# Token-major b, k and v of an RWKV-7 mixer by 32x32 blocks on VectorE, with a different spacing of steps

## The chip, the core and the metric

The kernel runs on one core of a Trainium2 chip. TensorE (PE) multiplies, VectorE (DVE), ScalarE (ACT) and GpSimd (POOL) work on tiles in SBUF, SyncE (SP) issues loads. The metric is device microseconds of one execution, the median over the runs; lower is better.

## The reference

One layer of a decoder: an input projection feeds two mixers that run side by side, a sliding-window attention and an RWKV-7 time mixing; both are projected, gated and merged, and a SwiGLU feed-forward follows. All is float32, with 2048 tokens and 16 meta tokens, width 1024.

```python
u = rms_norm(h, norm_mix_g); proj = u @ w_in + b_in
y_attn = sliding_window_sink_attention(partial_rope(q), partial_rope(k), v, sinks)
y_rwkv = rwkv7_time_mix(p_rwkv, ...)
merged = gates[..., :D] * (y_attn @ w_br_attn) + gates[..., D:] * (y_rwkv @ w_br_rwkv)
h = h + merged @ w_o
f = rms_norm(h, norm_ffn_g)
h = h + (silu(f @ w_gate) * (f @ w_up)) @ w_down
# inside rwkv7_time_mix, for each token and head, with state S (64x64):
sa = S a_t
S = S * w_t + sa b_t + v_t k_t ;  y = S r_t
```

## The kernel before

**The dense work.** The 2048 tokens go in four blocks of 512. `phase_a(b)` makes the input projection, `phase_c(b)` the branch projections (`pb`), the output projection (`ph_o`), the feed-forward (`pg`, `pu`) and its return (`ph_d`). Each float32 product is made of three matmuls of 128x512. TensorE executes its instructions in the order in which the program issues them (`InOrder`); the other engines' queues are ordered by a scheduler when the program is built.

**The mixers** are Python generators that `tick()` moves on by one step (one `yield`) after every few dense matmuls. One step of one unit stands for about 18 dense matmuls on TensorE's queue. An RWKV unit `rwkv(i, j)` treats 256 tokens (four chunks of 64) of two heads; there are 32, and one for the meta tokens. A unit starts `LAG` = 14 steps after the one before it. Attention units `attn(ti)` treat 128 tokens of all heads and run one after another.

**What an RWKV unit does**, in the order of its steps: loads and shifts `rkv`; makes decays (`pc`, `pe`, `pi`) and the block-diagonal operand `bkd` (b and k, feature-major, written by VectorE at L730 and L731); makes the chunk matrices `pg` on TensorE; sends one of them through DRAM (`lt_d`, `lt`) to GpSimd, which inverts it in 62 operations (L772, L774, the tiles `pr` and `xv`). Then it turns `bkd` and v token-major: 8 transposes on TensorE into `pb`, which ScalarE copies to `bt`, and 2 into `pvv`, which VectorE and ScalarE copy to the block-diagonal `vd`. After `WAIT_INV` steps the inverses return through DRAM (`xt_d`, then `td`), VectorE turns two blocks of them (`tq`, L808), and TensorE completes them (`pq`, `pq2`) and runs the recurrence over the four chunks (`ch`, with `ud` and `sd` on VectorE, `rd` and `yt` on ScalarE). At the end `yt` is normalised, turned (`pyt`) and stored to `y_d`.

**What an attention unit does**: loads q, k, v and the rotated copies `qr`, `kr` by SP; one step later GpSimd rotates them (L945 to L947, and `roped`), `set_keys` splits the keys into `kw`, and `parts(0)` splits q into `qs` on ScalarE and VectorE (L955, L956); two steps later TensorE turns v (`pv`) and makes the scores (`psS`).

Of the kernel before, what the change touches and what calls it, by code (L numbers as in the profile page):

```python
# [19 lines left out]
F32 = mybir.dt.float32  # L20
F32R = mybir.dt.float32r
AF = mybir.ActivationFunctionType
# [5 lines left out]
P = 128  # L28
# [19 lines left out]
WAIT_INV = 9  # L48
# [30 lines left out]
def layer(ctx, tc, x, meta, w_in, w_br, w_o, w_gate, w_up, w_down, w2a, a2, g2, vecs, sinks, gfin,  # L79
          consts, rope, out):  # L80
    nc = tc.nc
    V, A, G, S = nc.vector, nc.scalar, nc.gpsimd, nc.sync
# [18 lines left out]
    T = InOrder()  # L101
# [8 lines left out]
    cp = pool("const")  # L110
    dp = pool("dram", space=DRAM)
    dn = pool("dense")
    mx = pool("mixer")
    psd = pool("psd", bufs=3, space=PSUM)
    psg = pool("psg", bufs=4, space=PSUM)
    psc = pool("psc", bufs=1, space=PSUM)

    def f32(ap):
        return ap.bitcast(F32)
# [22 lines left out]
    ident = cc("ident")  # L142
# [407 lines left out]
    bkd = cp.tile([P, 2, 4, P], F32, name="bkd")  # L550
    vds = [cp.tile([P, 4, P], F32, name=f"vd{q}") for q in range(2)]
    td = cp.tile([P, 4, P], F32, name="td")
    rd = cp.tile([P, P], F32, name="rd")
    ud = cp.tile([P, P], F32, name="ud")
    for t in (bkd, *vds, td, rd):
        G.memset(t, 0.0)
    gmask = cst[:, _CC["gstrict"][0]:_CC["gincl"][1]]

# [56 lines left out]
    n = TU // CH  # L615

    def rwkv(i, j):
# [3 lines left out]
        m = i is None  # L621
        uid = 4 * NU if m else 4 * i + j
        nm = f"{i}_{j}"
        t1 = lambda s, b=1: mx.tile([P, TU], F32, tag=s, bufs=b, name=f"{s}_{nm}")
        cv = lambda ap: ap.rearrange("p (c t) -> p c t", t=CH)
# [17 lines left out]
        rm, km, vm = (rkv[:, q] for q in range(3))  # L643
# [84 lines left out]
        for h in range(2):  # L728
            hb = slice(64 * h, 64 * h + 64)
# [13 lines left out]
        for x in range(2):  # L743
            pg = psg.tile([P, 512], F32, tag="pg", name=f"pg_{nm}_{x}")
# [29 lines left out]
            G.tensor_add(xv[:, :, r + 1:], xv[:, :, r + 1:], pr[:, :, :n_])  # L774
        yield

        bt = mx.tile([P, 2, n, P], F32, tag="bt", bufs=2, name=f"bt_{nm}")
        vd = vds[(uid + m) % 2]
        for x in range(2):
            pb = psg.tile([P, 512], F32, tag="pg", name=f"pb_{nm}_{x}")  # L780
            for c in range(n):
                T.transpose(pb[:, c * P:(c + 1) * P], bkd[:, x, c], ident)
            A.activation(bt[:, x], pb.rearrange("p (c f) -> p c f", f=P), AF.Copy)
            if x == 0:
                yield
        pvv = psg.tile([P, 512], F32, tag="pg", name=f"pvv_{nm}")
        for t in range(2):
            T.transpose(pvv[:, t * P:(t + 1) * P], vm[:, t * P:(t + 1) * P], ident)
        pvt = pvv[:, :2 * P].rearrange("p (t f) -> p t f", f=P)
        for q in range(2):  # L790
            for h in range(2):
                hb, qb = slice(64 * h, 64 * h + 64), slice(64 * q, 64 * q + 64)
                if q == h:
                    V.tensor_copy(vd[hb, q::2, hb], pvt[qb, :, hb])
                else:
                    A.activation(vd[hb, q::2, hb], pvt[qb, :, hb], AF.Copy)
        for _ in range(WAIT_INV):
            yield
        G.dma_start(xt_d[uid].rearrange("m (b c) i -> b m (c i)", c=4), xv.rearrange("p c i -> p (c i)"))
        lo, hi = [slice(64 * h, 64 * h + 32) for h in range(2)], [slice(64 * h + 32, 64 * h + 64) for h in range(2)]  # L800
        for h in range(2):
            for q, r32 in ((0, lo[h]), (1, hi[h])):
# [21 lines left out]
        for c in range(n):  # L824
# [8 lines left out]
            for h in range(2):  # L833
                hb = slice(64 * h, 64 * h + 64)
# [45 lines left out]
    def set_keys(k, cols):  # L880
        for g in range(2):
            gb = slice(64 * g, 64 * g + 64)
            for d in (gb, slice(64 - 64 * g, 128 - 64 * g)):
                A.activation(kw[d, g, 0, cols], k[gb], AF.Copy)
                V.tensor_sub(kw[d, g, 1, cols], k[gb], f32(kw[gb, g, 0, cols]))
# [6 lines left out]
    def roped(o, src, rot, cs, w, name):  # L892

        G.tensor_mul(src, src, cs[:, 0])
        G.tensor_mul(rot, rot, cs[:, 1])
        G.tensor_add(o, src, rot)
# [28 lines left out]
    def attn(ti):  # L925
# [7 lines left out]
        q = mx.tile([P, 4, P], F32, tag="q", bufs=1, name=f"q_{ti}")  # L933
# [6 lines left out]
        load_rot(kr, 4, 1, c0, P)  # L940
        vt = mx.tile([P, P], F32, tag="vl", bufs=1, name=f"vl_{ti}")
        S.dma_start(vt, proj_d[5][:, c0:c0 + P])
        yield
        b4 = lambda k: cs[:, k].unsqueeze(1).to_broadcast([P, 4, P])
        G.tensor_mul(q, q, b4(0))  # L945
        G.tensor_mul(qr, qr, b4(1))
        G.tensor_add(q, q, qr)  # L947
        roped(kl[:, 0], kl[:, 0], kr[:, 0], cs, P, ti)
        set_keys(kl[:, 0], own)

        def parts(g):
# [14 lines left out]
        for g in range(2):  # L966
            gb = slice(64 * g, 64 * g + 64)
            nm = f"{ti}_{g}"
# [58 lines left out]
    def tick():  # L1027

        turn[0] = (turn[0] + 1) % TURNS
        rs = [u for u in units if u[2] == "r"]  # L1030
        for u in list(units):
            if turn[0] != (0 if u[2] == "a" else 1 if len(rs) > 1 and u is rs[0] else 2):
                continue
            u[1] += 1
            if next(u[0], 0) == 0:
                units.remove(u)
        if todo_r and turn[0] == 2:
            i, j = todo_r[0]
            b = (i or 0) // 2
            young = min((u[1] for u in units if u[2] == "r"), default=LAG)  # L1040
            if young >= LAG - 3 and i not in asked and set(range(6, 9)) <= emitted[b]:
                asked.add(i)
                start("l", lora(i), b)
            if young >= LAG and i in loras and set(
                    range(9, 21) if i is None else range(PAIR0 + 3 * j, PAIR0 + 3 * j + 3)) <= emitted[b]:
                todo_r.pop(0)
                start("r", rwkv(i, j), b)
        if todo_a and turn[0] == 0 and not any(u[2] == "a" for u in units):
            ti = todo_a[0]
            b = (ti or 0) // 4  # L1050
            if set(range(6)) <= emitted[b]:
                todo_a.pop(0)
                start("a", attn_meta() if ti is None else attn(ti), b)
# [135 lines left out]
```

## Time and profile before

| | us |
|---|---|
| median of 3 runs (3372.03 to 3376.8) | 3375.84 |
| the profiled execution, its own time | 3377.94 |
| its span | 3376.0 |
| PE busy | 3256.3 (96%) |
| DVE busy | 1542.1 (46%) |
| ACT busy | 1163.2 (34%) |
| POOL busy | 1156.1 (34%) |

TensorE is busy in nearly the whole span; its idle time lies in waits that the trace names, and after a longer wait its granted clock is halved for a few microseconds.

### The profile page before, as it was taken

Reading aid. Unit: us, or ns where it says so; the run is one execution under the profiler, and the core shown is the slowest. Engines: PE = TensorE matmul, PEld = TensorE weight load, DVE = VectorE, ACT = ScalarE, POOL = GpSimd, SP = SyncE. Lnnn points to the kernel's source line nnn. Section 1 sums busy time; section 2 is a strip of 40 time slices with the busy share of each in tenths; the row PEclk is TensorE's granted clock in tenths of the full one; section 3 lists DMA queues with packets and bytes.
Section 4 is the critical chain, followed back from the end, with each engine's and each line's share of the span. In section 5 each row is a group of like instructions: output and inputs, shape, how many; then the busy total and the mean of one; then the engine's idle time right before and its main releaser. Section 6 shows DMA issues by size and latency. Waiting matters only on the chain.

```text
span 3376.0 us, 47237 instructions
## 1 busy us (share of the span) xinstructions
PE 3256.3 (96%) x16909; PEld 2681.2 (79%) x16909; DVE 1542.1 (46%) x3622; ACT 1163.2 (34%) x2863; POOL 1156.1 (34%) x2771
## 2 busy tenths in 40 slices
PE   7899999999999998999999999999999999999998
PEld 6777887787888777887787788887888888778887
DVE  3343233232332585666666644445654443542233
ACT  4354344443443455445443422233242221220001
POOL 1124434334344454554453433444333341000000
PEclk9999999999999999999999999999999999999999
DMA  7777666676666776666668555556755555855555
GB/s 262 273 261 241 209 226 211 190 227 197 223 210 215 242 260 206 234 235 234 231 237 280 176 170 174 179 181 201 263 171 177 171 177 176 288 179 191 196 191 181
DMA packets 229448, 721.46 MB, mean 214 GB/s; under 512 B 36333, under 2 KB 90989, under 8 KB 168286
## 3 DMA queue, kind: packets, MB, share of 16 engines
q1 hardware_dynamic: 158126, 516.15, 47.1%
q0 software_dynamic: 38736, 154.99, 12.9%
q10 hardware_dynamic: 32352, 47.31, 3.8%
q8 instruction: 133, 2.18, 0.3%
q14 instruction: 101, 0.83, 0.1%
HBM read 533.46 MB, written 184.82 MB: 213 GB/s over the span
## 4 chain that ended last, share of the span: by engine, by line
PE 60%; DMA 6%; DVE 3%; POOL 3%; ACT 2%; issue 2%; SPq 0%; POOLq 0%; DVEq 0%; ACTq 0%
PE pg L93 14%; PE pu L93 12%; PE ph_d L93 11%; PE pi L93 6%; PE pb L93 4%; PE ch L93 4%; PE ph_o L93 3%; DMA yl<-y_d 1%; PE ph_o_l L93 1%; POOL pr L772 1%; POOL xv L774 1%; DMA lt<-lt_d 1%; PE py L93 1%; PE pq L93 1%; DVE h L202 1%
## 5 line engine op out<-in xcount | busy, mean ns | idle before, releaser
L93 PE MATMUL pi<-act_u,w_in 128*128 128x512 f32 x3552 | 902.5, 402 | 10.5 <-DVE m L202 6.1
L93 PEld LDWEIGHTS pi<-act_u,w_in 128*128 128x128 f32 x3552 | 652.9, 191 | 144.0 <-issue 5.5
L93 PE MATMUL pg<-act_f,w_g 128*128 128x512 f32 x2112 | 533.7, 399 | 6.8 <-DVE act_f L202 6.8
L93 PE MATMUL pu<-act_f,w_u 128*128 128x512 f32 x2112 | 522.9, 395 | 0.0
L93 PE MATMUL ph_d<-w_d,mg_g 128*128 128x512 f32 x1920 | 472.5, 397 | 10.4 <-DVE h L202 10.0
L93 PEld LDWEIGHTS pg<-act_f,w_g 128*128 128x128 f32 x2112 | 388.4, 189 | 85.3 <-DVE act_f L202 9.0
L93 PEld LDWEIGHTS pu<-act_f,w_u 128*128 128x128 f32 x2112 | 388.9, 188 | 78.8 <-issue 1.0
L93 PEld LDWEIGHTS ph_d<-w_d,mg_g 128*128 128x128 f32 x1920 | 355.5, 189 | 85.9 <-DVE h L202 14.5
L772 POOL TENSOR_TENSOR pr<-xv,lt 128x124 f32<-128x124 f32 (+30 forms) x992 | 330.5, 333 | 248.9 <-DMA lt<-lt_d 176.8
L774 POOL TENSOR_TENSOR xv<-xv,pr 128x124 f32<-128x124 f32 (+30 forms) x992 | 341.1, 344 | 74.5
L202 DVE SCALAR_TENSOR_TENSOR h<-ph_d,h 128x512 f32<-128x512 f32 x320 | 218.9, 689 | 130.0 <-PE ph_d L93 128.3
L93 PE MATMUL pb<-ya,w_br 128*128 128x512 f32 x768 | 191.0, 400 | 1.0 <-DMA w_br<-wd_br 0.6
L93 PEld LDWEIGHTS pb<-ya,w_br 128*128 128x128 f32 x768 | 143.1, 191 | 30.9 <-DVE mg_m L202 1.0
L202 DVE SCALAR_TENSOR_TENSOR th<-th,pg 128x512 f32<-128x512 f32 x88 | 60.4, 687 | 214.6 <-ACT th L202 214.5
L93 PE MATMUL ph_o<-w_o,mg_m 128*128 128x512 f32 x576 | 144.2, 400 | 6.8 <-DVE h L202 3.8
L804 POOL DMA_DIRECT2D td<-xt_d x132 | 72.6, 557 | 225.4 <-PE ch L93 197.3
L202 ACT ACTIVATE th<-pg 128x512 f32<-128x512 f32 x88 | 52.6, 598 | 281.4 <-PE pg L93 281.0
L202 DVE TENSOR_TENSOR th<-th,pu 128x512 f32<-128x512 f32 x88 | 60.5, 687 | 183.8 <-PE pu L93 183.3
L243 POOL TENSOR_TENSOR ss_o<-ss_o,mhalf 128x1 f32<-128x1 f32 x16 | 9.4, 590 | 372.5 <-DVE ss_o L202 372.3
L755 POOL DMA_DIRECT2D lt_d<-g x128 | 71.2, 561 | 184.0 <-DVE g L750 182.0
L202 ACT ACTIVATE mg_g<-th 128x512 fp32r<-128x512 f32 x88 | 55.3, 628 | 222.6 <-DVE th L202 222.5
L93 PEld LDWEIGHTS ph_o<-w_o,mg_m 128*128 128x128 f32 x576 | 106.5, 190 | 31.3 <-DVE h L202 5.2
(356 smaller groups left out, 4512.1 us busy)
## 6 DMA issues: line engine op xcount, KB each, us to landing
w_in<-wd_in SPq DMA_DIRECT2D x111, 1024.0 KB, 5.5
w_g<-wd_g SPq DMA_DIRECT2D x66, 1024.0 KB, 5.0
w_u<-wd_u SPq DMA_DIRECT2D x66, 1024.0 KB, 5.0
w_d<-wd_d SPq DMA_DIRECT2D x60, 1024.0 KB, 5.0
wd_in<-w_in POOLq DMA_DIRECT2D x37, 1024.0 KB, 5.8
w_br<-wd_br SPq DMA_DIRECT2D x24, 1024.0 KB, 7.0
wd_g<-w_g POOLq DMA_DIRECT2D x22, 1024.0 KB, 5.2
wd_u<-w_u POOLq DMA_DIRECT2D x22, 1024.0 KB, 5.3
```

Of the source, the lines that this page charges most:

```text
L93: r = f(*p, **k)
L202: return f(*p, **k)
L243: G.tensor_tensor(ss[:rows, 3:4], ss[:rows, 2:3], mhalf[:rows, 0:1], op=ALU.pow)
L755: G.dma_start(lt_d[uid, m0:m0 + n].rearrange("c j i -> j c i"), g[r32, :, 0, o])
L772: G.tensor_mul(pr[:, :, :n_], xv[:, :, r:r + 1].to_broadcast([P, 4, n_]), lt[:, r, r + 1:].unsqueeze(1).to_broadcast([P, 4, n_]))
L774: G.tensor_add(xv[:, :, r + 1:], xv[:, :, r + 1:], pr[:, :, :n_])
L804: G.dma_start(td[r32, :, r32], xt_d[uid, m0:m0 + 4].rearrange("m j i -> j m i"))
```

## The change

The ten TensorE transposes of a unit and the copies out of PSUM are replaced by `V.transpose` of 32x32 blocks from SBUF to SBUF: 8 instructions for v and 16 for b and k, each over four chunks (32 partitions, 4x32 elements). `bt` becomes two fixed, zeroed tiles `bts`, used in turn. The step ahead of each half of `bt` stays within the unit's count up to the store of the inverses, and one step is added between that store and the loads of `td`. In the attention one step is added between the loads and the rotation, and two between the rotation and `set_keys` with `parts(0)`.

```diff
-    for t in (bkd, *vds, td, rd):
+    bts = [cp.tile([P, 2, 4, P], F32, name=f"bt{q}") for q in range(2)]
+    for t in (bkd, *vds, td, rd, *bts):
         G.memset(t, 0.0)
...
-        bt = mx.tile([P, 2, n, P], F32, tag="bt", bufs=2, name=f"bt_{nm}")
-        vd = vds[(uid + m) % 2]
+        bt, vd = bts[(uid + m) % 2], vds[(uid + m) % 2]
+        vc4 = cv(vm)
+        for h in range(2):
+            for r in range(2):
+                for q in range(2):
+                    rb, qb = (slice(64 * h + 32 * z, 64 * h + 32 * z + 32) for z in (r, q))
+                    V.transpose(vd[qb, :, rb], vc4[rb, :, 32 * q:32 * q + 32])
         for x in range(2):
-            pb = psg.tile([P, 512], F32, tag="pg", name=f"pb_{nm}_{x}")
-            for c in range(n):
-                T.transpose(pb[:, c * P:(c + 1) * P], bkd[:, x, c], ident)
-            A.activation(bt[:, x], pb.rearrange("p (c f) -> p c f", f=P), AF.Copy)
-            if x == 0:
-                yield
-        pvv = psg.tile([P, 512], F32, tag="pg", name=f"pvv_{nm}")
-        for t in range(2):
-            T.transpose(pvv[:, t * P:(t + 1) * P], vm[:, t * P:(t + 1) * P], ident)
-        pvt = pvv[:, :2 * P].rearrange("p (t f) -> p t f", f=P)
-        for q in range(2):
+            yield
             for h in range(2):
-                hb, qb = slice(64 * h, 64 * h + 64), slice(64 * q, 64 * q + 64)
-                if q == h:
-                    V.tensor_copy(vd[hb, q::2, hb], pvt[qb, :, hb])
-                else:
-                    A.activation(vd[hb, q::2, hb], pvt[qb, :, hb], AF.Copy)
-        for _ in range(WAIT_INV):
+                for r in range(2):
+                    for q in range(2):
+                        rb, qb = (slice(64 * h + 32 * z, 64 * h + 32 * z + 32) for z in (r, q))
+                        V.transpose(bt[qb, x, :, rb], bkd[rb, x, :, qb])
+        for _ in range(WAIT_INV - 1):
             yield
         G.dma_start(xt_d[uid].rearrange("m (b c) i -> b m (c i)", c=4), xv.rearrange("p c i -> p (c i)"))
+        yield
...
         S.dma_start(vt, proj_d[5][:, c0:c0 + P])
-        yield
+        for _ in range(2):
+            yield
...
         roped(kl[:, 0], kl[:, 0], kr[:, 0], cs, P, ti)
+        for _ in range(2):
+            yield
         set_keys(kl[:, 0], own)
```

**Place 1, TensorE's queue where unit (4, 3) makes its chunk matrices `pg`.** Unit (4, 2) is the one before it; `ph_o1` is dense work of block 1. Before:

```order
L93 MATMUL pb_1_7_1_18743<-ya_1_7_17969,w_br_1_7_18704 128x512 x3
L93 MATMUL ph_o1_7_0_0_18764<-w_o1_7_0_18762,mg_m1_4_18450 128x512 x3
L93 MATMUL pq2_4_2_0_18768<-td_118,tq_4_2_18656 32x32 x4
L93 MATMUL pq2_4_2_1_18769<-td_118,tq_4_2_18656 32x32 x4
L93 MATMUL ch_4_2_0_18782<-vd0_116,g_4_2_1_18083 128x128
L93 MATMUL ch_4_2_0_18782<-sd2_109,ar_4_2_17891 128x128
L93 MATMUL ch_4_2_0_18782<-vd0_116,bt_4_2_18218 128x128
L93 MATMUL pg_4_3_0_18790<-ar_4_3_18673,bkd_115 128x128 x4
L93 MATMUL pg_4_3_1_18802<-ar_4_3_18673,bkd_115 128x128 x4
```

Now:

```order
L93 MATMUL pb_1_7_1_18647<-ya_1_7_17785,w_br_1_7_18623 128x512 x3
L93 MATMUL ph_o1_7_0_0_18686<-w_o1_7_0_18684,mg_m1_4_18335 128x512 x3
L93 MATMUL pq_4_2_0_18690<-tq_4_2_18639,g_4_2_0_17872 32x32 x4
L93 MATMUL pq_4_2_1_18691<-tq_4_2_18639,g_4_2_0_17872 32x32 x4
L93 MATMUL pg_4_3_0_18702<-ar_4_3_18581,bkd_115 128x128 x4
L93 MATMUL pg_4_3_1_18714<-ar_4_3_18581,bkd_115 128x128 x4
```

From `pq` on, a unit stands one step later against the unit behind it: `pq` of (4, 2) now stands where its `pq2` stood, 36 dense matmuls behind `pc` of (4, 3) and no longer 18.

**Place 2, VectorE's queue where unit (4, 3) writes `bkd`.** `tq_4_2` are the two blocks of the unit before, for which `pq` of place 1 waits; `gst` and `yt` belong to unit (4, 1), `ptm` to the attention, `mt` to the dense work. Before:

```order
L808 STREAM_TRANSPOSE tq_4_2_18656<-td_118 32x128
L855 TENSOR_SCALAR gst_4_1_18710<-gst_4_1_18710 128x4
L723 TENSOR_TENSOR bv_4_3_18669<-rkv_4_3_18438,pbo_4_3_18666 128x256
L727 TENSOR_TENSOR ar_4_3_18673<-kn_4_3_18480,pe_4_3_18662 128x4x64
L732 TENSOR_TENSOR ar_4_3_18673<-rkv_4_3_18438,pe_4_3_18662 128x4x64
L734 COPY fc_4_3_18680<-pe_4_3_18662 128x4
L738 COPY pe0_4_3_18683<-pe_4_3_18662 128x1
L730 TENSOR_TENSOR bkd_115<-tw_4_3_18671,pi_4_3_18664 64x4x64
L731 TENSOR_TENSOR bkd_115<-kp_4_3_18552,pi_4_3_18664 64x4x64
L730 TENSOR_TENSOR bkd_115<-tw_4_3_18671,pi_4_3_18664 64x4x64
L731 TENSOR_TENSOR bkd_115<-kp_4_3_18552,pi_4_3_18664 64x4x64
```

Now:

```order
L732 TENSOR_TENSOR bkd_115<-kp_4_3_18459,pi_4_3_18572 64x4x64
L737 TENSOR_TENSOR fc_4_3_18588<-pe_4_3_18570 128x3
L819 TENSOR_SCALAR sd3_110<-sd3_110,pe0_4_3_18591 128x128
L1007 TENSOR_TENSOR ptm_14_1_18608<-ppm_14_1_18606,cst_80 128x512
L792 STREAM_TRANSPOSE bt1_122<-bkd_115 32x4x32 x4
L202 SCALAR_TENSOR_TENSOR mt_1_6_1_18613<-tg_1_6_1_18538,pb_1_6_1_18559 128x512
L792 STREAM_TRANSPOSE bt1_122<-bkd_115 32x4x32 x8
L842 SCALAR_TENSOR_TENSOR sd1_108<-ch_4_1_3_18510,fc_4_1_16794,sf_4_1_3_18516 128x128
L805 STREAM_TRANSPOSE tq_4_2_18639<-td_118 32x128 x2
L792 STREAM_TRANSPOSE bt1_122<-bkd_115 32x4x32 x2
L202 TENSOR_TENSOR mt_1_6_0_18557<-mt_1_6_0_18557,mt_1_6_1_18613 128x512
L792 STREAM_TRANSPOSE bt1_122<-bkd_115 32x4x32 x2
```

The scheduler puts most of the 16 transposes of `bkd` right behind its last write, and the older unit's `tq` behind 12 of them; before, `tq` stood ahead of `bkd`.

**Place 3, GpSimd's queue where attention unit 7 rotates q.** `pr` and `xv` are the inversion of an RWKV unit, with the operation's number behind the unit's. Before:

```order
L774 TENSOR_TENSOR xv_1_2_7705<-xv_1_2_7705,pr_1_2_4_7719 128x4x27
L772 TENSOR_TENSOR pr_1_2_5_7722<-xv_1_2_7705,lt_1_2_7703 128x4x26
L774 TENSOR_TENSOR xv_1_2_7705<-xv_1_2_7705,pr_1_2_5_7722 128x4x26
L772 TENSOR_TENSOR pr_1_2_6_7725<-xv_1_2_7705,lt_1_2_7703 128x4x25
L945 TENSOR_TENSOR q_7_7853<-q_7_7853,cs_7_7851 128x512
L774 TENSOR_TENSOR xv_1_2_7705<-xv_1_2_7705,pr_1_2_6_7725 128x4x25
L947 TENSOR_TENSOR q_7_7853<-q_7_7853,qr_7_7854 128x512
L772 TENSOR_TENSOR pr_1_2_7_7728<-xv_1_2_7705,lt_1_2_7703 128x4x24
```

Now:

```order
L773 TENSOR_TENSOR pr_1_3_30_8464<-xv_1_3_8372,lt_1_3_8370 128x4
L892 TENSOR_TENSOR kr_7_8861<-kr_7_8861,cs_7_8851 128x128
L775 TENSOR_TENSOR xv_1_3_8372<-xv_1_3_8372,pr_1_3_30_8464 128x4
L893 TENSOR_TENSOR kl_7_8860<-kl_7_8860,kr_7_8861 128x128
L795 DMA xt_d_79<-xv_1_3_8372 8x16x128
L769 DMA xv_2_0_9153<-in_consts 128x128
L943 TENSOR_TENSOR q_7_8853<-q_7_8853,cs_7_8851 128x512
L945 TENSOR_TENSOR q_7_8853<-q_7_8853,qr_7_8854 128x512
```

The rotation stood after the seventh of 31 rounds of the inversion of unit (1, 2), with `psS` of this attention unit 81 dense matmuls behind `pg` of (1, 2) on TensorE's queue; now it stands behind the whole inversion of (1, 3), and `psS` 264 dense matmuls behind that unit's `pg`.

## Rows read from the trace of the kernel before

**Rows 1.** The page, busy time of each engine, its share of the span, instructions

```profile
PE 3256.3 (96%) x16909; PEld 2681.2 (79%) x16909; DVE 1542.1 (46%) x3622; ACT 1163.2 (34%) x2863; POOL 1156.1 (34%) x2771
```

**Rows 2.** Waits of PE: what it waited for, us in total, times, longest

```profile
PE psS L93 <- DVE qs L956: 27.3, 9, 5.8
...
PE ph_d L93 <- DVE h L202: 10.0, 7, 4.5
PE psS L93 <- ACT kw L884: 7.1, 1, 7.1
PE pq L93 <- DVE tq L808: 6.9, 2, 5.2
...
PE ph_o L93 <- DVE h L202: 3.8, 2, 3.3
```

**Rows 3.** Groups by line and form on PE: busy, mean ns; the unit's transposes

```profile
L93 PE MATMUL pb<-cst,bkd 128*128 128x128 f32 x256 | 38.8, 275 | 0.0
...
L93 PE MATMUL pvv<-cst,rkv 128*128 128x128 f32 x64 | 12.2, 273 | 0.0
```

**Rows 4.** Timeline of PE, one burst of four transposes: start, length, instructions

```profile
2549.71 0.60 PE L93 MATMUL pb<-cst,bkd 128*128 128x128 f32 x4
```

**Rows 5.** Groups on ACT and DVE: the copies that empty those PSUM tiles

```profile
L783 ACT ACTIVATE bt<-pb 128x512 f32<-128x512 f32 x64 | 38.2, 596 | 120.9 <-PE pb L93 120.9
...
L796 ACT ACTIVATE vd<-pvv 64x128 f32<-64x128 f32 x64 | 17.4, 272 | 2.4 <-DVE vd L794 1.6
...
L794 DVE COPY vd<-pvv 64x128 f32<-64x128 f32 x64 | 18.4, 288 | 26.8 <-ACT vd L796 15.1 <-PE pvv L93 10.8
```

**Rows 6.** DVE, the only 32x32 transposes of before: their group, and one pair in the timeline

```profile
L808 DVE STREAM_TRANSPOSE tq<-td 32x128 f32<-32x128 f32 x64 | 19.0, 297 | 20.3 <-DMA td<-xt_d 19.2
...
2019.15 0.62 DVE L808 STREAM_TRANSPOSE tq<-td 32x128 f32<-32x128 f32 x2
```

**Rows 7.** Timeline of DVE and PE about one write of `bkd`

```profile
2535.07 0.41 DVE L730 TENSOR_TENSOR bkd<-tw,pi 64x256 f32<-64x256 f32 x1
2535.41 0.41 DVE L731 TENSOR_TENSOR bkd<-kp,pi 64x256 f32<-64x256 f32 x1
2535.83 0.42 DVE L730 TENSOR_TENSOR bkd<-tw,pi 64x256 f32<-64x256 f32 x1
2536.17 0.42 DVE L731 TENSOR_TENSOR bkd<-kp,pi 64x256 f32<-64x256 f32 x1
...
2532.47 0.61 PE L93 MATMUL pc<-cst,sig 128*128 128x130 f32 x4
...
2533.15 4.24 PE L93 MATMUL ph_d<-w_d,mg_g 128*128 128x512 f32 x18
...
2542.28 0.59 PE L93 MATMUL pq<-td,tq 32*32 32x32 f32 x16
```

**Rows 8.** Windows: length, then busy (instructions) of PE, PEld, DVE, ACT, POOL, clock, DMA

```profile
1097.20:1860.00 762.80, 728.37 (x3842) 595.17 (x3841) 501.25 (x1144) 356.54 (x885) 370.71 (x799) 0.98 0.71 240
```

**Rows 9.** Timeline of all engines up to one late `psS`, in brackets idle and releaser

```profile
836.50 1.26 POOL L947 TENSOR_TENSOR q<-q,qr 128x512 f32<-128x512 f32 x1
...
839.19 1.27 PE L93 MATMUL psS<-kw,qs 128*128 128x272 f32 x4 [5.67 <-DVE qs L956]
```

**Rows 10.** Windows of 2.5 us behind such a wait, columns as in rows 8

```profile
637.50:640.00 2.50, 2.50 (x9) 2.11 (x9) 1.68 (x8) 0.00 (x0) 1.29 (x2) 0.50 0.10 31
...
645.00:647.50 2.50, 2.50 (x14) 2.13 (x13) 1.73 (x6) 1.32 (x2) 0.00 (x0) 1.00 0.00 0
```

**Rows 11.** Timeline at the start of block 3's branch projection

```profile
2895.10 0.38 PE L93 MATMUL pyt<-cst,yt 128*128 128x128 f32 x2
...
2901.77 0.32 SPq L426 DMA_DIRECT2D yl<-y_d  x1
...
2906.69 0.69 DVE L202 TENSOR_TENSOR ya<-yl,ya 128x512 fp32r<-128x512 f32 x1 [2.97 <-ACT ya L202]
...
2908.79 3.45 PE L93 MATMUL pb<-ya,w_br 128*128 128x512 f32 x14 [0.36 <-DVE h L202]
```

## The prediction

> **What bounds the kernel now.** I read the page first: TensorE is busy 96% of the span, VectorE 46%, ScalarE and GpSimd 34% each [rows 1]. So time is won only by taking work off TensorE or by ending its waits. The list of TensorE's waits came next [rows 2]. Its largest entry is `psS`, the attention's scores, which waits for the split q (`qs`, VectorE) nine times and for the split keys once: 27.3 + 7.1 = 34.4 us. All others on which this change bears are smaller: the dense accumulations that wait for VectorE's `h` (10.0 and 3.8) and `pq` that waits for `tq` (6.9). Then I read the timeline and the windows around single cases, below, and the order of the queues before and after the change.
>
> **Transposes off TensorE.** The groups on TensorE have 256 transposes into `pb` and 64 into `pvv` [rows 3]; the meta unit has ten more, so 330 go. Their mean of 275 ns is a duration with overlap, not a price. A burst of four took 0.60 us [rows 4], so each further one costs (600 - 275) / 3 = 108 ns, and 330 x 108 ns = 36 us. From both sides: 28 us if about a fifth of them stand where TensorE would wait anyway, 52 us if their busy time [rows 3] were their whole price. I take 36, since the matmuls around a burst follow it without idle time. The 64 + 64 copies on ScalarE and the 64 on VectorE that emptied PSUM go too, 38.2 + 17.4 and 18.4 us [rows 5]. ScalarE also no longer stands 120.9 us idle in its queue waiting for `pb`. I count nothing for ScalarE: at a third of the span it is covered by TensorE's dense matmuls. Without that cover it could give at most a few us, which I leave in the range.
>
> **Transposes onto VectorE.** A unit gets 8 + 16 = 24 of them. The only such instruction of before, L808, takes 297 ns for the same 128 elements in 32 partitions, and a pair of them 0.62 us [rows 6], so the second starts about 0.32 us after the first. Other VectorE instructions overlap: the first two writes of `bkd` start 0.34 us apart at 0.41 us each, but the third, which changes from partitions 0-63 to 64-127, starts 0.42 us after the second, at its end [rows 7]. Most of the 24 change their partitions against the instruction before, as the pair of L808 does, so I take 0.32 us: 7.7 us a unit, 254 us for 33 units. If they overlapped like the first two writes, it would be about 0.22 us, 5.3 us a unit.
>
> The Trainium skill, "VectorE: DVE Perf Modes", section "Two Vector instructions with no wait between them", says that an instruction whose input or output starts in another 32-partition quadrant than the one before it is held until all earlier ones have finished. The two rows of before agree. By that rule it is 0.32, and otherwise 0.22 us, the third rival below.
>
> Busy time on VectorE rises by 792 x 297 ns - 18.4 us = 217 us, to 52%. What matters is who waits in its queue.
>
> *The older unit's* `tq`. Place 2 of the order shows `tq` now behind up to 16 of the transposes of the next unit's `bkd`; `pq` on TensorE waits for it, and all dense matmuls queue behind `pq`. In one unit `pc` starts at 2532.47 and the last write of `bkd` ends at 2536.59, 4.1 us later [rows 7]. `pq` stands 36 dense matmuls behind `pc` after the change, where `pq2` (`pq<-td,tq`) stood: 2542.28, 9.8 us behind `pc`. So 5.7 us are there. With 10 transposes and the pair of `tq` VectorE needs 3.2 + 0.6 and about 1 us of small work between them, in time; with 16 it needs 5.1 + 0.6 + 0.6 = 6.3, which is 0.6 us late, and each dense `h` or `th` in between adds 0.6. I went through the new order of all 32 units so: about ten units come late, by 0.4 to 5 us, some 24 us in all; the longer ones fall where other bursts also push `pq` back, so I take +21, with the clock's share. Bounds: 3 us (half of what `pq` waits for now goes and nothing comes) and 60 (nearly 2 us at each unit).
>
> *The dense accumulations.* Where weights are split for the first time, VectorE is busy 501 of 763 us [rows 8], 66%. The added 217 us fall into some 2500 us of mixers, so about 66 us fall here: 74%. If a queue's wait grows as u / (1 - u), from 1.9 to 2.8, the 13.8 us of waits for `h` [rows 2] grow by half, +7; with the clock I take +10. Bounds 0 (the bursts fall between evictions) and 30 (the wait triples).
>
> **The steps of the attention.** In one late case GpSimd finishes the rotated q at 837.76, held up by the inversion's operations; `qs` follows, and TensorE starts `psS` at 839.19 after 5.67 us of idle time [rows 9]. In place 3 of the order the rotation stands inside an inversion of GpSimd, `psS` 81 dense matmuls (at 4.24 us for 18 [rows 7] about 19 us) behind the start of that unit's `pg`; now it stands behind a whole inversion, `psS` 264 matmuls (62 us) behind. I compared all 16 attention units: before, six of them rotate within an inversion with `psS` 63 to 153 matmuls behind its `pg`; after the change five do, but each with far more matmuls per operation passed. Loads to `psS` is 108 matmuls instead of 54, some 13 us more, and the longest wait is 7.1 us. So nearly all 34.4 us end.
>
> A wait also costs the clock: behind the longest of them on `qs`, 5.8 us, the granted clock was 0.50, and TensorE issued 9 matmuls in 2.5 us, against 14 at 1.00 [rows 10]. Five of 14 in one window and as much in part of the next is 0.9 to 1.8 us. At about 1 us for each of the ten waits (an estimate from those rows) it is 10 us. Of 44 us I take 42, bounds 20 (half the units still late through VectorE's queue) and 48.
>
> What is late next in the attention is nothing that TensorE waits for: it ends later, but each of its blocks is needed only at that block's branch projection, hundreds of dense matmuls on.
>
> **The step at the inverses.** The store of the inverses stays at its step; the loads of `td` and all behind move by one, 18 dense matmuls. SP's queue gets nothing new. GpSimd's loads of `td` are four issues that now come a step after the store, and the older unit's last use of `td` moves as much, so that wait is unchanged: 0, bounds -3 and +3. At the end the last unit finishes 4.2 us later against block 3's branch projection. There the load of its y is issued 6.7 us after `pyt` [rows 11], the last `ya` is done at 2907.4, and the matmuls that begin at 2908.79 come to it: a slack of 1.4 us or somewhat more, against 4.2, and SP holds the next weights behind that load. +3, bounds 0 and 7.
>
> **Sum.** 3376.0 - 36 - 42 + 21 + 10 + 3 = 3332 us of span. The profiled execution's own time is 2 us over its span and 2 us over the median, so the median after should be 3332 too.
>
> **The rivals.** *VectorE too late for every unit (slower).* Without the `pq` term the sum is -65 us; 32 units eat that up at 2.0 us each. The present 6.9 us, 5.2 of them at once, show that a late `tq` does stop TensorE [rows 2]. At 3 us a unit, clock included, it gives 3376 - 65 + 96 = 3407. Against it: `pq` stands 18 matmuls later than before. The same page of the Trainium skill, section "Rules for kernel authors", speaks for this rival: it gives a 128x128 transpose to TensorE where PSUM will do, and asks for few VectorE instructions. By rows it is 10 x 108 ns = 1.1 us of TensorE against 7.7 us of VectorE a unit; no run of before shows them side by side.
>
> *The attention's waits stay.* `qs` also queues on VectorE; if that is what makes it late, only 8 of the 44 us come: 3376 - 36 - 8 + 21 + 13 = 3366.
>
> *The transposes overlap.* At 0.22 us 16 of them take 3.5 us, `tq` is in time nearly always (+4), the dense wait grows less (+6): 3376 - 36 - 42 + 4 + 6 + 3 = 3311.
>
> **How the numbers follow.** My forecast has 0.66, with its own range 3300 to 3358; VectorE too late 0.12; waits stay 0.10; overlap 0.12. The range 3298 to 3368 holds the first, the third and the fourth but for their tails, and leaves out the slower case. A change under 0.2% (6.7 us) can't be told from none here. Faster 0.84, within 0.2% 0.05, slower 0.11: the slower case nearly whole is the last, the tails of it and of the waits that stay are the middle.
>
> **What would show it.** No matmuls `pb<-cst,bkd` and `pvv`, TensorE's busy time down by some 40 us; 792 more transposes on VectorE with starts 0.3 us apart; `psS <- qs` gone from the top of TensorE's waits; `pq <- tq` at some 20 us instead of 6.9, with ten or so waits. It is wrong if `pq` waits at nearly every unit, if `psS` still waits over 15 us, or if TensorE waits for `h` much over 20.

## The result and the profile after

The changed kernel takes 3393.01 us (median of 4 runs, 3389.67 to 3400.67) against 3376.32 us: ratio 1.0054, 95% interval [1.0032, 1.0075]. It is slower by 0.5%; 3332 us was forecast, and the range of 3298 to 3368 did not hold the time.

The page's first line shows that the exchange itself took place: 330 matmuls fewer on TensorE, 792 transposes more and 66 copies fewer on VectorE, which is now at 52%, as forecast [rows 1].

```profile
PE 3238.4 (95%) x16579; PEld 2655.8 (78%) x16579; DVE 1768.7 (52%) x4348; ACT 1108.2 (33%) x2731; POOL 1168.4 (34%) x2773
```

With the mean granted clock of each of the two profiled executions (the view of the cores) the difference of their spans splits into three parts. First the kernel before, then the one after: span, clock.

```profile
core 0: 3376.0 us, clock 0.987
```

```profile
core 0: 3394.0 us, clock 0.983
```

What the clock took is, as an estimate, (1 - 0.987) x 3376 = 44 us before and 58 after: +14 (the clock has three digits, so each is good to about 2 us). Without that, TensorE's busy time is 3256.3 - 44 = 3212 and 3238.4 - 58 = 3181: -32, which is what the 330 transposes were worth (97 ns each). The same working puts the six runs below that keep all transposes on TensorE at 3210 to 3216 us, and those that have all of them on VectorE at 3169 to 3184: 28 to 43 us less than before. The rest of the span is idle time: 3376.0 - 3256.3 = 120 before, 156 after: +36. Together -32 + 14 + 36 = +18, the difference of the spans.

The list of TensorE's waits after (us in total, times, longest) shows where the idle time is:

```profile
PE pq L93 <- DVE tq L805: 16.4, 10, 3.1
PE ph_d L93 <- DVE h L202: 15.4, 12, 6.3
...
PE pt_u L93 <- DVE act_u L202: 9.9, 5, 6.1
PE ch L93 <- ACT rd L832: 7.8, 4, 4.6
PE ph_o_l L93 <- DVE h L202: 7.3, 2, 4.3
...
PE ph_d L93 <- DVE th L202: 6.0, 3, 3.2
PE ph_d_l L93 <- DVE h L202: 5.6, 4, 2.1
...
PE pg L93 <- ACT tq L811: 5.3, 5, 2.4
PE ph_o L93 <- DVE mt L202: 4.9, 3, 3.4
PE pb L93 <- ACT ya L202: 4.4, 1, 4.4
...
PE psS L93 <- DVE ms L975: 3.1, 1, 3.1
```

The waits of `psS` on `qs` and `kw` [rows 2] are gone, as forecast. In their place stand some 70 us of other waits. Summed by the engine that ended them, 48 of these end with VectorE (63 us before without `qs`, 111 now): `tq`, `h`, `act_u` (the input of the projection), `th` (the hidden of the feed-forward), `ms` (the maxima of the attention). Another 18 end with ScalarE (`rd`, `ya`, and `tq` at L811; `kw` left out) and 4 with loads. What the transposes do shows best against all_steps (below), which has the new steps but leaves the transposes on TensorE: there 62 us end with VectorE and 30 with ScalarE, here 111 and 30.

The groups on VectorE show the new instructions at the length that L808 had [rows 6]:

```profile
L792 DVE STREAM_TRANSPOSE bt<-bkd 32x128 f32<-32x128 f32 x528 | 158.0, 301 | 7.5
L785 DVE STREAM_TRANSPOSE vd<-rkv 32x128 f32<-32x128 f32 x256 | 77.4, 302 | 15.5 <-PE ch L93 7.7 <-PE ch_None L93 4.3
```

Now one unit in the timeline: from the last write of `bkd` to `pq` of the unit before it.

```profile
2395.30 0.42 DVE L732 TENSOR_TENSOR bkd<-kp,pi 64x256 f32<-64x256 f32 x1
2396.63 2.17 DVE L792 STREAM_TRANSPOSE bt<-bkd 32x128 f32<-32x128 f32 x7
...
2399.22 1.91 DVE L792 STREAM_TRANSPOSE bt<-bkd 32x128 f32<-32x128 f32 x6
...
2401.16 0.69 DVE L202 SCALAR_TENSOR_TENSOR mt<-tg,pb 128x512 f32<-128x512 f32 x1
...
2401.90 1.65 PE L93 MATMUL ph_o<-w_o,mg_m 128*128 128x512 f32 x6 [0.37 <-DVE mt L202]
2402.21 0.30 DVE L805 STREAM_TRANSPOSE tq<-td 32x128 f32<-32x128 f32 x1
2402.54 0.63 DVE L792 STREAM_TRANSPOSE bt<-bkd 32x128 f32<-32x128 f32 x2
2403.20 0.69 DVE L202 SCALAR_TENSOR_TENSOR h<-ph_o,h 128x512 f32<-128x512 f32 x1
2403.48 0.43 PE L93 MATMUL pq<-tq,g 32*32 32x32 f32 x8
...
2405.44 0.30 DVE L805 STREAM_TRANSPOSE tq<-td 32x128 f32<-32x128 f32 x1
...
2405.80 0.43 PE L93 MATMUL pq<-tq,g 32*32 32x32 f32 x8 [1.88 <-DVE tq L805]
```

The transposes begin 0.9 us behind the last write of `bkd`, which over all 33 units is also the median; the median of the last one's end is 7.1 us. `mt`, `h` and both halves of `tq` queue among them. VectorE stood idle only 7.5 us in all ahead of the 528 transposes of `bkd` (the last figure of their group above), so it is not they that wait. The pace is visible too: six transposes in 1.91 us are one each 0.32 us, the price that the prediction took. In the program's order each writes another 32 partitions than the one before it. The section of the Trainium skill that the prediction named ("VectorE: DVE Perf Modes", "Two Vector instructions with no wait between them") holds such an instruction until the earlier ones have finished; the trace agrees.

### The profile page after: what moved, and what is told of

Its sections match the earlier page's. It is cut to its first block, busy times and chain, and to the rows that moved or that the text cites. A ratio compares the mean times of both kernels' runs of the same rounds, so it can differ in the third digit from the quotient of the medians.

```text
span 3394.0 us, 47151 instructions
## 1 busy us (share of the span) xinstructions
PE 3238.4 (95%) x16579; PEld 2655.8 (78%) x16579; DVE 1768.7 (52%) x4348; ACT 1108.2 (33%) x2731; POOL 1168.4 (34%) x2773
## 4 chain that ended last, share of the span: by engine, by line
PE 62%; DVE 12%; DMA 12%; POOL 7%; issue 4%; ACT 3%; SPq 0%; ACTq 0%; POOLq 0%; DVEq 0%
PE pi L93 15%; PE pg L93 12%; PE pu L93 11%; PE ph_d L93 9%; PE ch L93 4%; PE pb L93 3%; PE ph_o L93 2%; DVE bt L792 2%; POOL pr L773 2%; POOL xv L775 2%; DMA wr_in<-in_w_in 2%; DMA lt<-lt_d 2%; DVE h L202 2%; PE py L93 1%; DMA wr_g<-in_w_gate 1%
## 5 line engine op out<-in xcount | busy, mean ns | idle before, releaser
L93 PE MATMUL pi<-act_u,w_in 128*128 128x512 f32 x3552 | 896.4, 402 | 16.1 <-DVE m L202 6.1
L773 POOL TENSOR_TENSOR pr<-xv,lt 128x124 f32<-128x124 f32 (+30 forms) x992 | 338.4, 341 | 298.5 <-DMA lt<-lt_d 227.0
L792 DVE STREAM_TRANSPOSE bt<-bkd 32x128 f32<-32x128 f32 x528 | 158.0, 301 | 7.5
L844 ACT ACTIVATE yt<-ch 64x128 f32<-64x128 f32 x128 | 34.9, 273 | 309.9 <-DVE sd L842 304.1
```

The lines of the kernel that those rows point to most:

```text
L93: r = f(*p, **k)
L773: G.tensor_mul(pr[:, :, :n_], xv[:, :, r:r + 1].to_broadcast([P, 4, n_]), lt[:, r, r + 1:].unsqueeze(1).to_broadcast([P, 4, n_]))
L792: V.transpose(bt[qb, x, :, rb], bkd[rb, x, :, qb])
L844: A.activation(yt[64 * (c % 2):64 * (c % 2) + 64, c // 2], see[64:128], AF.Copy)
```

## The experiments

Each was timed in rounds with the kernel before on the same chip. The last column puts each ratio on one scale, against 3376 us; its interval reaches 4 to 7 us to either side.

| run | us | ratio to before, 95% | against before |
|---|---|---|---|
| attn_steps | 3352.40 | 0.9943 [0.9930, 0.9956] | -19 |
| td_step | 3350.67 | 0.9936 [0.9924, 0.9947] | -22 |
| later_store | 3348.87 | 0.9923 [0.9909, 0.9938] | -26 |
| all_steps | 3346.12 | 0.9922 [0.9907, 0.9937] | -26 |
| dve_transposes | 3404.03 | 1.0090 [1.0075, 1.0106] | +30 |
| the changed kernel | 3393.01 | 1.0054 [1.0032, 1.0075] | +18 |
| twice | 3505.26 | 1.0385 [1.0364, 1.0405] | +130 |
| wide_eight | 3357.69 | 0.9946 [0.9927, 0.9965] | -18 |
| v_only | 3349.28 | 0.9924 [0.9903, 0.9945] | -26 |
| spread_fours | 3326.46 | 0.9854 [0.9833, 0.9874] | -49 |
| ordered_eights | 3329.59 | 0.9867 [0.9853, 0.9882] | -45 |
| ordered_block24 | 3363.03 | 0.9959 [0.9942, 0.9975] | -14 |
| wide_spread | 3327.25 | 0.9857 [0.9844, 0.9870] | -48 |
| spread_old_steps | 3358.50 | 0.9949 [0.9934, 0.9963] | -17 |
| idle_at_bkd | 3382.31 | 1.0017 [1.0004, 1.0030] | +6 |
| idle_later | 3374.69 | 0.9988 [0.9976, 1.0000] | -4 |

### Which part costs: the steps or the transposes

Theory A: the transposes on VectorE make its other chains late. Theory B: the steps only move the waits. Theory C: the step at the inverses costs.

**attn_steps**, the attention's part of the diff alone.

> Only the three steps in the attention are added; the ten transposes of a unit stay on TensorE and the inverses keep their step. Theory A (the new VectorE transposes make the other chains of VectorE late, the steps do what the prediction said): the 34 us of psS waits on qs and kw end and part of their clock comes back, so 3376 - 34 - 5 = about 3337 us, ratio 0.988, PE's idle time 111 - 34 = 77 us. Theory B (the waits only move: whatever stands where psS stood meets other late chains): idle time stays at 100 us or more and the time within 10 us of 3376, ratio 0.997 to 1.003.

**td_step**, the kernel before and one line:

```diff
         G.dma_start(xt_d[uid].rearrange("m (b c) i -> b m (c i)", c=4), xv.rearrange("p c i -> p (c i)"))
+        yield
```

> Only the step between the store of the inverses and the loads of td is added; everything else as before. Theory C (pq of a unit now stands directly ahead of pg of the next, both need the four small PSUM buffers): pg waits for ScalarE's tq in several units, +15 to +25 us, ratio 1.005 to 1.007. Theories A and B: within 7 us of 3376, ratio 0.998 to 1.002; pq's waits for tq fall a little.

**all_steps**, both of these.

> All steps of the change, attention and inverses, with the ten transposes left on TensorE: what is missing to the changed kernel is then VectorE's transposes alone. Theory A: about as attn_steps, 3337 us, ratio 0.988, so the transposes on VectorE cost 3393 - 3337 = some 55 us net. Theory B: 3376 or above. Theory C: attn_steps + 20 = 3357, ratio 0.994.

**dve_transposes**, the changed kernel without these steps.

> Only the transposes go to VectorE; the attention's steps and the step at the inverses are those of before. Theory A: TensorE's work falls by 31 to 36 us, but waits of chains through VectorE (tq, h, act_u, th, rd) grow by about 70 us and the clock by 13: 3376 - 34 + 80 = about 3420 us, ratio 1.013, and psS still waits some 34 us. Theory B: the transposes are near neutral or gain, 3376 - 34 + 20 = 3362, ratio 0.996, since it is the steps that cost. Theory C (the step at the inverses puts pq next to pg and costs some 20 us): like B here.

The steps gain and the transposes lose, with either set of steps: B and C fall. Theory A holds in kind, with sizes that were too large: it had 3420 us for dve_transposes, where 3404 came, and 3337 for all_steps, where 3346 came. TensorE's waits of attn_steps show why it gained 19 and not 39. None on `qs` or `kw` is left, but these are new:

```profile
PE ch L93 <- DVE ud L840: 6.1, 4, 4.0
...
PE psS L93 <- ACT vz L967: 5.4, 1, 5.4
```

That td_step gained was in no theory. Half of the time that the attention waits for `qs` ends there too, and `pq` hardly waits for `tq` any more [rows 2]:

```profile
PE psS L93 <- DVE qs L957: 13.8, 8, 3.5
...
PE psS L93 <- ACT kw L885: 7.2, 1, 7.2
...
PE pq L93 <- DVE tq L809: 1.0, 1, 1.0
```

Its clock is 0.991 instead of 0.987, 14 us by itself. Both parts end waits on `qs`, so together they gain 26 and not 41.

**later_store** asks whether td_step gains because GpSimd no longer issues the loads of `td` directly behind the store, or because the unit's later part moved.

```diff
-        for _ in range(WAIT_INV):
+        for _ in range(WAIT_INV + 1):
```

> The kernel before with the added step ahead of the store of the inverses and not behind it: everything from the store on moves by one step, and the loads of td are issued directly behind the store again. If td_step's 23 us came from the unit's later part moving against the unit behind it (pq where pq2 stood) and against the attention: the same here, 3351 us, ratio 0.994. If they came from GpSimd not standing between the store and the loads of td: none of it, 3376 us, ratio 1.000.

It gains as much, so the spacing of GpSimd's issues is not the reason: it is the move of the later part by 18 dense matmuls. Whether its new place against the unit behind or against the attention makes the difference was not tested.

### How the cost grows, and what removes it

In the changed kernel TensorE idles 109 us in waits of over 0.3 us between 300 and 2950 us, 65 times. For 29 of these waits (46 us), more than a tenth of the 5 us up to their end went into transposes on VectorE.

**v_only**: `all_steps`, with the diff's eight transposes for `vd` in place of `pvv`.

> All steps of the change, only v (8 transposes a unit) on VectorE; b and k stay on TensorE and ScalarE. The start is all_steps, 3346 us; TensorE gains 66 x 108 ns = 7 us. A2 (cost in proportion to VectorE's time): a third of some 80 us, 3346 - 7 + 27 = 3366, ratio 0.998. A1 (blocks): a block of 8 is 2.5 us and holds back little, 3346 - 7 + 10 = about 3349, ratio 0.993.

**twice**: each `V.transpose` of the change issued twice in a row.

> The changed kernel with every VectorE transpose issued twice in a row, 48 a unit, blocks up to 32 long and VectorE at 59%. If VectorE's time is what costs, in proportion, another 80 us: about 3475 us, ratio 1.029. If blocks are what costs, and a wait grows faster than in proportion with the block's length, more: 3500 us or above, ratio 1.037. If VectorE is not the cause at all, within 10 us of 3393.

**wide_eight**: one instruction for b and k.

```diff
-                        V.transpose(bt[qb, x, :, rb], bkd[rb, x, :, qb])
+            V.transpose(bt[qb, :, :, rb], bkd[rb, :, :, qb])
```

> The changed kernel with b and k of a block turned by one instruction of 256 elements a partition, 8 instructions instead of 16, in one step. If the price of such an instruction is half fixed, VectorE spends some 1.5 us a unit less, and a block is 3.6 instead of 5 us long. Theory A1: the longest blocks shrink by a third, 3393 - 15 = about 3378 us, ratio 1.001. Theory A2: 50 of 254 us of VectorE time go, a fifth of the cost of 65 to 80 us, also about 3378. If 256 elements take twice the time, no change: 3393.

**spread_fours**: six groups of four, one a step; `late` is to keep an instruction in the program's order on its queue.

```diff
+        for g in range(6):
+            for rb, qb in quads[4 * (g % 2):4 * (g % 2) + 4]:
+                if g < 2:
+                    o = qb.start % 64
+                    late(V.transpose(vd[qb, :, rb], vc4[rb, :, o:o + 32]))
+                else:
+                    late(V.transpose(bt[qb, g // 2 - 1, :, rb], bkd[rb, g // 2 - 1, :, qb]))
+            if g < 5:
+                yield
```

> The changed kernel with the same 24 transposes of a unit, but cut into six groups of four, one group a step and kept in the program's order on VectorE, so that they no longer stand 8 to 16 together. Theory A1 (the blocks are what makes other chains late: in the changed kernel 46 of 109 us of TensorE's idle time between 300 and 2950 us stand behind 5 us of VectorE with many transposes): about 40 us of waits and 10 to 18 us of clock come back, 3393 - 55 = about 3340 us, ratio 0.990. Theory A2 (VectorE's total time, 52% instead of 46%, is what costs, wherever it stands): within 10 us of 3393, ratio 1.003 to 1.008.

The cost of the transposes on VectorE is the difference to all_steps and the 32 us that TensorE saved: for the changed kernel 18 + 26 + 32 = 76 us, for spread_fours -49 + 26 + 32 = 9, for wide_eight 40, for twice 188. For v_only it is 6 with a fifth of the 32 us, and about 1 with what TensorE's busy time shows in its own trace. With the intervals and the 28 to 43 us above, each is good to some 10 us. So eight a unit cost at most some 6 us, 24 cost 76 and 48 cost 188: more than in proportion. And the same VectorE time, spread, costs 9. A2 falls. A wide transpose of 256 elements takes 433 ns, not 2 x 301. That is the half fixed price that the expectation of wide_eight assumed, so it doesn't explain why 36 us were gained where 15 were expected; that stays open.

```profile
L788 DVE STREAM_TRANSPOSE bt<-bkd 32x256 f32<-32x256 f32 x264 | 114.2, 433 | 6.5 <-PE ch L93 3.2
```

The same unit in windows of 8 us behind the last write of `bkd` (columns as in [rows 8]), first in the changed kernel, then in spread_fours:

```profile
2395.72:2403.72 8.00, 6.04 (x31) 4.13 (x30) 7.57 (x24) 0.67 (x2) 0.00 (x0) 1.00 1.02 376
2403.72:2411.72 8.00, 6.12 (x47) 5.30 (x44) 6.78 (x16) 1.58 (x4) 3.21 (x5) 1.00 0.31 91
```

```profile
2346.64:2354.64 8.00, 6.95 (x48) 5.62 (x47) 6.73 (x18) 2.26 (x6) 1.04 (x1) 1.00 1.01 399
2354.64:2362.64 8.00, 8.00 (x58) 6.69 (x57) 3.86 (x7) 0.97 (x4) 2.23 (x5) 1.00 0.50 163
```

VectorE (the third engine) is busy 7.57 and 6.78 of 8 us in the first, and TensorE only 6.04 and 6.12; in the second VectorE has more room, 6.73 and 3.86, and TensorE loses 1.05 us in all.

### Length of the blocks, order, or place

**ordered_eights**: the diff's three groups of eight at their steps, only with `late`. **ordered_block24**: these 24 in one step, with `late`.

> The changed kernel with its three groups of eight at the steps where its text has them, but kept in the program's order on VectorE. Theory A1a (the length of a block decides; spread_fours at 3326 us had four, the changed kernel at 3393 up to sixteen): blocks of 8 are 2.5 us, between the two, about 3345 us, ratio 0.991. Theory A1b (what helped in spread_fours is only that the transposes no longer stand ahead of tq and of urgent evictions, whatever their number): as spread_fours, 3326 us, ratio 0.985.

> All 24 transposes of a unit in one step, kept in the program's order: VectorE's time is that of spread_fours to the instruction, only the blocks are 24 long, some 7.5 us. Theory A1a: worse than the changed kernel, since nearly any chain that falls into a block waits: 3393 + 20 to + 60, about 3430 us, ratio 1.016. Theory A1b (order, not length): near spread_fours, 3326 to 3345. Theory A2 (total time) is out already and would say 3326 too.

**wide_spread**: spread_fours with the wide form for b and k, four groups of two.

> spread_fours with b and k of a block in one instruction of 256 elements (433 ns instead of two of 301): six groups, two of four for v and four of two for b and k. VectorE spends 49 us less and no block is longer than 1.3 us. By theory A1a the remaining waits behind blocks (30 us with many transposes before them) shrink a little: 3326 - 8 = about 3318 us, ratio 0.982. If spread_fours already has all that there is: 3326.

At the same VectorE time, in order, blocks of 4, 8 and 24 cost 9, 13 and 44 us; 9 and 13 can't be told apart here. So length counts, but ordered_block24 is faster than the changed kernel, whose uninterrupted runs are 16 at most: order or place must count as well. With `late` the first transpose of `bt` stands 19.6 us (median) behind the last write of `bkd` in ordered_eights, and 0.9 us without. `late` did not move the group for v there: in both kernels its eight begin 10 us (median) ahead of the end of that write, since they need only v. So ordered_eights differs from the changed kernel by the 16 of b and k alone, and in ordered_block24 the eight of v stand in the block too. wide_spread gives nothing more.

**early_eights** was to put the groups in order right behind `bkd`.

> The groups of eight of ordered_eights, kept in the program's order too, but moved to the place that they have in the changed kernel: b and k's first eight directly behind the last write of bkd, the second eight a step later, v's another step later. VectorE's time and the blocks are those of ordered_eights (3330 us). Theory P (the place right behind bkd is what costs, since the chains of this unit and of the unit before it come through VectorE there): most of the 63 us come back, 3370 to 3395 us, ratio 0.998 to 1.005. Theory O (what costs is that the scheduler places the transposes freely, wherever the place): about 3330 us, ratio 0.987.

It took 3490.84 us (ratio 1.0348 [1.0328, 1.0368]) and settles nothing: issued there, a unit's b, k are in the program's order written ahead of the last reads of `bt` by the unit two before it, which so reads others' values, and TensorE has a wait that the changed kernel doesn't have:

```profile
PE ch L93 <- DVE bt L745: 112.5, 30, 7.3
```

**idle_at_bkd** and **idle_later** replace it: all_steps with twelve VectorE operations a unit that nobody reads. They begin at the last write of `bkd` in the first and 26 us behind it (median) in the second, where they stand behind a `yield` after `vd`.

```diff
+        for k in range(12):
+            late(V.tensor_reduce(idle[:, k], cc("amask")[:, :256].rearrange("p (c t) -> p c t", t=64), axis=AX.X, op=ALU.add))
```

> all_steps (transposes on TensorE, 3346 us) with twelve VectorE reductions of a constant a unit, 0.42 us each, 5 us together, that nobody reads, directly behind the last write of bkd, where the changed kernel has its transposes. Theory P (that place costs): half or more of the cost of the 24 transposes there (83 us with blocks), + 40 to + 60, about 3395 us, ratio 1.005. Theory L (only the length of a block counts, wherever it is): as idle_later.

> The same twelve idle reductions a unit in one block, 5 us of VectorE, but five steps, some 20 us, later, where the program's text has the transposes. Theory P: well under idle_at_bkd; by ordered_block24, whose 7.5 us block costs 3363 - 3346 + 36 = 53 us there, 5 us cost some 25 to 35: about 3376 us, ratio 1.000, 20 us under idle_at_bkd. Theory L: within 8 us of idle_at_bkd.

The first is 10 us slower than the second (0.0029 of the time, about 0.001 to 0.005, so 3 to 17 us), the twelve taking 4.1 us of VectorE. So the place costs, half of the 20 us that theory P said; the 8 us that theory L allowed lie in the interval too. Against all_steps the two cost 32 and 22 us: one block costs even at the later place. Where the idle time falls is clearer. First idle_at_bkd, then idle_later:

```profile
PE pq L93 <- DVE tq L812: 11.6, 8, 4.0
```

```profile
PE ch L93 <- ACT yt L852: 14.5, 7, 5.6
```

From the timelines, over the 33 last writes of `bkd`: VectorE's mean share, and TensorE's idle us (each wait in the stretch in which it ends), in the stretches of 8 us behind them.

| | VectorE 0-8 | 8-16 | 16-24 | 24-32 | TensorE idle 0-8 | 8-16 | 16-24 | 24-32 |
|---|---|---|---|---|---|---|---|---|
| the kernel before | 0.49 | 0.41 | 0.46 | 0.40 | 16.1 | 8.6 | 3.0 | 5.4 |
| all_steps | 0.68 | 0.41 | 0.40 | 0.42 | 7.1 | 2.0 | 1.4 | 5.3 |
| the changed kernel | 0.94 | 0.63 | 0.37 | 0.42 | 29.3 | 15.7 | 3.4 | 13.8 |
| ordered_eights | 0.69 | 0.45 | 0.60 | 0.67 | 6.2 | 5.8 | 3.7 | 9.7 |
| ordered_block24 | 0.70 | 0.43 | 0.64 | 0.80 | 7.6 | 1.5 | 2.0 | 33.8 |
| idle_at_bkd | 0.93 | 0.55 | 0.39 | 0.46 | 32.4 | 2.9 | 1.8 | 2.7 |
| idle_later | 0.69 | 0.43 | 0.41 | 0.72 | 3.9 | 3.2 | 1.7 | 7.3 |

Behind `bkd` VectorE is the busiest already: the new steps take it from 49% to 68%, with less idle time of TensorE, and the changed kernel fills it to 94%. There TensorE's idle time grows, by 22 + 14 us against all_steps in the first two stretches; idle_at_bkd shows +25 in the first and +1 in the second, with nothing changed but 4 us of VectorE.

**spread_old_steps**: spread_fours with the steps of before.

> The spread transposes alone, with the steps of before in the attention and at the inverses. With the steps they cost VectorE 3326 - 3346 + 36 = 16 us against TensorE's 36. If steps and transposes add up: 3376 - 20 = 3356 us, ratio 0.994, psS still waiting some 34 us. If the steps are needed for the transposes to gain (tq and qs late behind them as in dve_transposes): 3376 or more.

3358.5 us: within the noise, steps and well-placed transposes add up (-17 and -26, against -49).

## Why the prediction was wrong

The sum was -36 - 42 + 21 + 10 + 3 = -44 us; it came out at +18.

**Transposes off TensorE**: right. -32 by TensorE's busy time (28 to 43 over the runs), -36 forecast.

**The steps of the attention and the step at the inverses**: right in sign, too large by 13 together: -26 against -42 + 3. All 34.4 us of these `psS` waits ended, but alone this gave 19: TensorE's idle time fell only by 20 (119.7 to 100.0 in the profiles), as other waits came up, `psS` for `vz`, the turned v (5.4), and `ch` for `ud` (6.1) among them. The step at the inverses, put at 0 to +3, gave 22 alone; I had asked only what its loads of `td` wait for, not what the unit's later part meets when it moves.

**Transposes onto VectorE**: the duration was right. The failed step is the price of the waits behind them in VectorE's queue, +31 in two terms, where the experiments give 76. *The older unit's `tq`* was nearly right: ten waits of 16.4 us in all, longest 3.1, where some 24 in ten units were worked out. *The dense accumulations* failed (+10, bounds 0 and 30): I spread the new 217 us evenly, had VectorE's mean share rise from 66% to 74% and scaled the waits for `h` alone. But Place 2 of the order already showed that the transposes stand together behind `bkd`. There the share is 94%. TensorE waits longer for `h`, 28.8 us on `ph_d`, `ph_o_l`, `ph_d_l` and `ph_o` against 15.1 on the same four before (13.8 in [rows 2], 1.3 on `ph_d_l`); that is the third of the signs of being wrong that the prediction named. And other chains through VectorE wait that did not before: `pt_u` for `act_u`, `ph_d` for `th`, `psS` for `ms`, `pg` for `tq`, 24.3 us together. The clock, counted as a gain, lost 14 us in the profiled pair.

**Block 3's start**: `pb` waits 4.4 us for `ya`, +3 forecast.

**The rivals.** "VectorE too late for every unit" was nearest, with 3407, and right that VectorE's queue decides, but not by `pq` at every unit: that wait came ten times. That its time came near is luck. "The transposes overlap" is out by the 0.32 us, "the attention's waits stay" by their end. The Trainium skill's rule that spoke for the slower case ("VectorE: DVE Perf Modes", "Rules for kernel authors": a 128x128 transpose to TensorE, few VectorE instructions) fits the changed kernel. It doesn't fit spread_fours, which is some 20 us faster than all_steps with as many VectorE instructions as the changed kernel.

**What stays open.** Of the 76 us, 13 remain in ordered_eights, where only the 16 transposes of b and k have moved. So about 63 come from where these stand, and among what. The idle pair prices the place alone at 10 us (3 to 17) for a block of 4.1 us, and such a block right behind `bkd` at 32 in all; the 16 transposes there take 5.0 us and cost some 70. That the rest is the free order, with `tq`'s two halves apart among transposes as in the timeline, is argued and not shown.

## What to carry to other kernels

Work moved to an engine at half load is not free because the mean leaves room: look up where the scheduler puts it, and read that engine's share in the few microseconds there, with all chains that pass. If an order can be kept, cut such work into pieces of about 1 to 2.5 us, well behind that engine's busiest stretch: here that turned 3393 into 3326 us with as many transposes. And test each part of a change alone; two of the three parts here gained, and the third, as it was placed, hid it.

## What the runs showed of the hardware

A 32x32-block transpose of 256 elements a partition takes 433 ns against 301 for 128, so by these two sizes some 170 ns of it do not grow with the size (an estimate); wide_spread, which uses it in small groups, was no faster for it (3327 us against 3326). A transpose of 128x128 on TensorE, in bursts of two and four, was worth 97 ns (28 to 43 us for 330 over the runs), a third of its recorded 275 ns.
